# RWKV mixer: a 64x64 triangular inverse by 16x16 substitution and two joins, masks in Vector's evictions, products moved between engines

## The chip, the core and the metric

The kernel runs on one core of one Trainium2 chip. A core has five engines that run their own instruction streams and wait for each other by semaphores: TensorE (PE in the rows; its weight loads are PEld), VectorE (DVE), ScalarE (ACT), GpSimdE (POOL) and SyncE (SP), which here only issues DMA transfers. Data lie in SBUF, and matmuls write to PSUM, which has 8 banks of 128x512 fp32. The metric is the device time of one execution in microseconds; less is better.

## The reference, cut to what matters

The program is two layers of a sequence model on a 256x1024 fp32 input. Eight stages follow each other: ffn, gmlp, ffn, ple, ffn, **rwkv**, ffn, ple. Only the rwkv stage, an RWKV-7 time mixer with 16 heads of 64, is touched.

```python
dx = jnp.pad(h, ((0, 0), (1, 0), (0, 0)))[:, :-1] - h
x_rkv = h[:, :, None, :] + dx[:, :, None, :] * mu[:3]        # mixed inputs of r, k, v
r, k, v = split(einsum(x_rkv, w_in))
xw, xa, xg = h + dx * mu[3], h + dx * mu[4], h + dx * mu[5]
decay = exp(-exp(-softplus(-(w0 + tanh(xw @ w1) @ w2)) - 0.5))
a = sigmoid(a0 + (xa @ a1) @ a2)
g = sigmoid(xg @ g1) @ g2
kk = normalised per head (k * k_k);  k = k * (1 + (a - 1) * k_a)
def step(state, inp):                                         # per token
    sa = einsum('bhij,bhj->bhi', state, a_t)                  # a_t = -kk, b_t = kk * a
    state = state * w_t + sa b_t^T + v_t k_t^T
    y_t = einsum('bhij,bhj->bhi', state, r_t)
out = ((groupnorm(y) + sum(r * k * r_k) * v) * g) @ w_out
```

The kernel computes the recurrence in four chunks of 64 tokens. Inside a chunk the recurrence is a product with the inverse of a unit-triangular 64x64 matrix; there is one for each head and chunk, 64 in all.

## The kernel before

**Buffers.** SBUF holds 20 slots of 128x2048 fp32. `slot` takes one from a first-in first-out list and `drop` gives it back; `bank` and `unbank` do the same for the 8 PSUM banks. Whoever writes to a slot or bank waits until the last reader of its former content is done. The mixer's weights arrive as units of 1 MB, each a whole slot, by DMAs that SP issues in program order; `P(n, reserve)` prefetches while slots are free, `need` loads on demand. The weights of the stages around it arrive as `raw` and are split by ACT (L132) and by DVE or POOL (L134) into two parts.

**Order.** A scheduler of the framework places each instruction in its engine's stream, near the order in which the code is written. From then on each engine works strictly in that order.

**Names.** T = 256 tokens stand on the free axis of the transposed tiles (`hnT`, `kT`, `kk`, `av`, `tw`, `q2`, `bt`), the 1024 channels in 8 groups of 128 partitions. `xprod(n, ...)` (L785) makes mixed input n on DVE, in two slots that six inputs share in turn. `K` (L843) projects k, `knorm` (L864) and `kscale` (L879, POOL) make kk, `ktr` (L883) transposes k and kk, `low` (L927) makes the decay (`tw`) and the rate (`av`). `poly` (L950) turns `tw` into running decay products, two halves of 1024 columns, as a list of steps with two scans (L948) each, that the code hands out among the r projection's matmuls. POOL multiplies `bt = kk * av` (L1042) and `kT = kT * av` (L1055).

**The inverse.** `triangle(j)` (L1011, matmuls L1016) makes the off-diagonal products; their 32x32 diagonal blocks go to `md`, the blocks below to `mo`. One DVE transpose (L1061) lays them out so that each of 128 x 32 lanes has a row of its own, and `sub` (L1063) inverts the 32x32 blocks by substitution: for t = 1 to 31 a product (L1069) and a reduction (L1072), each split in up to three pieces. Two more transposes (L1229, L1232) bring the result to `wu` and `xx`. TensorE then joins the blocks to 64x64 by two sets of 64 matmuls of 32x32: q2 (L1250) and x2 (L1280).

**The v loop.** For each of 8 values of k, TensorE does four 128x512 matmuls of v (L1098) and the chunk-inner products of one channel group: 8 matmuls `sc` (L1113) and 8 `rb` (L1120). ACT copies each `sc` from its bank (L1114) and POOL multiplies it with the mask (L1115); the same for `rb` (L1122, L1124). The substitution runs beside it on DVE.

**Behind it.** `stack_v` (ACT, L1141/L1142) lays out v, `bonus` (L1149) makes r*k*v, `gate1` and `gate2` (L1190, L1208) project the gate, `tb` (L1257) transposes `bt` and `kt`. Then `chunk(c)` (L1297) runs four times: us, y, us, st, y, with gate2's eight matmuls put between.

## Time and profile before

| | us |
|---|---|
| median of 3 runs | 1233.63 (1231.42 to 1234.79) |
| the profiled execution, its own time | 1235.52 |
| its span in the trace | 1233.4 |
| TensorE busy, of the span | 1190.6 (97%) |
| VectorE busy | 805.5 (65%) |
| ScalarE busy | 610.4 (49%) |
| GpSimdE busy | 135.4 (11%) |
| mean granted TensorE clock | 0.98 |

The times in the rows count from the span's start. The mixer runs from about 750 to 980 us. TensorE is near its limit over the whole program, so the place to look at is where its busy share drops: the 40-slice line of the page shows 8, 8, 5 and 8 tenths in slices 27 to 30 (from 0), and the clock line 8, 7, 9 beside them. Every fp32 matmul leaves two records on PE, so "x64" in a row is 32 matmuls. A granted clock of 1.00 is 2.4 GHz and 0.50 is 1.2 GHz.

### The profile page before, as it was taken

The page shows a single profiled execution, that of the slowest core. Times are in us where ns is not written, and L with a number is a line of the kernel's source. Part 1 is how long each engine was busy: PE and PEld are TensorE (multiplying, and loading weights), DVE is VectorE, ACT ScalarE, POOL GpSimd, SP SyncE. Part 2 cuts the span into 40 slices and gives each one's busy share as a digit, 9 for nine tenths or more (in the row PEclk, how much of TensorE's full clock was granted, in tenths as well). Part 3 has the DMA queues.
Part 4 walks back from the last instruction along what each step waited for, and adds up shares of the span by engine and source line. Part 5 has one row for each costly group of instructions (what it writes and reads, how often), then busy time and mean ns, then how long its engine had stood idle before and what let it go on. Part 6 is the DMA issues. An engine that isn't in the chain of part 4 may idle for free.

```text
span 1233.4 us, 19738 instructions
## 1 busy us (share of the span) xinstructions
PE 1190.6 (97%) x7886; PEld 1023.4 (83%) x7886; DVE 805.5 (65%) x1214; ACT 610.4 (49%) x990; POOL 135.4 (11%) x133
## 2 busy tenths in 40 slices
PE   8999999999999999999999999988589899999997
PEld 7899998888889999987999996675357778999986
DVE  6776556696776556568656626599914988556563
ACT  7654446465574444478444412535154376444453
POOL 0000001000000000002000001343364420000011
PEclk9999999999999999999999999999879899999999
DMA  8875655565666555455656583011001358555510
GB/s 278 301 253 186 190 170 193 182 211 183 219 224 209 188 186 187 155 196 188 224 186 188 177 318 137 18 69 57 0 18 36 121 185 280 188 186 188 169 61 35
DMA packets 58780, 207.78 MB, mean 168 GB/s; under 512 B 6720, under 2 KB 7232, under 8 KB 58432
## 3 DMA queue, kind: packets, MB, share of 16 engines
q1 hardware_dynamic: 58688, 206.51, 50.4%
q8 instruction: 62, 1.02, 0.3%
q14 instruction: 30, 0.25, 0.1%
HBM read 205.44 MB, written 1.05 MB: 167 GB/s over the span
## 4 chain that ended last, share of the span: by engine, by line
PE 83%; DVE 10%; ACT 3%; issue 1%; DMA 1%; POOL 1%; SPq 0%; POOLq 0%; DVEq 0%; ACTq 0%
PE mm L157 13%; PE mm L158 13%; PE mm L156 13%; PE acc L156 8%; PE acc L157 8%; PE acc L158 8%; PE z L156 2%; PE z L157 2%; PE z L158 2%; DVE mx L1069 2%; PE k L855 2%; PE tr L253 1%; DMA raw<-in_w 1%; PE gate L156 1%; PE gate L157 1%
## 5 line engine op out<-in xcount | busy, mean ns | idle before, releaser
L134 DVE TENSOR_TENSOR w<-raw,w 128x1024 fp32r<-128x1024 f32 x335 | 408.1, 1223 | 252.6 <-ACT w L132 246.6
L132 ACT CAST w<-raw 128x1024 fp32r<-128x1024 f32 x340 | 356.6, 1052 | 319.1 <-PE mm L158 222.4
L156 PE MATMUL mm<-xT,w 128*128 128x256 f32 x1152 | 326.1, 283 | 0.0
L158 PE MATMUL mm<-xT,w 128*128 128x256 f32 x1152 | 326.0, 283 | 0.0
L157 PE MATMUL mm<-xT,w 128*128 128x256 f32 x1152 | 326.0, 283 | 0.0
L157 PEld LDWEIGHTS mm<-xT,w 128*128 128x128 f32 x1152 | 221.0, 192 | 1.3
L156 PEld LDWEIGHTS mm<-xT,w 128*128 128x128 f32 x1152 | 221.0, 192 | 1.3
L158 PEld LDWEIGHTS mm<-xT,w 128*128 128x128 f32 x1152 | 221.0, 192 | 0.0
L156 PE MATMUL acc<-w,hT 128*128 128x512 f32 x352 | 138.2, 393 | 0.0
L157 PE MATMUL acc<-w,hT 128*128 128x512 f32 x352 | 137.3, 390 | 0.0
L158 PE MATMUL acc<-w,hT 128*128 128x512 f32 x352 | 137.1, 390 | 0.0
L210 POOL TENSOR_SCALAR rpost<-ss 128x1 f32<-128x1 f32 x15 | 7.4, 494 | 790.2 <-ACT junk L217 790.2
L158 PEld LDWEIGHTS acc<-w,hT 128*128 128x128 f32 x352 | 66.1, 188 | 14.2
L156 PEld LDWEIGHTS acc<-w,hT 128*128 128x128 f32 x352 | 66.2, 188 | 12.6
L157 PEld LDWEIGHTS acc<-w,hT 128*128 128x128 f32 x352 | 66.2, 188 | 12.4
L379 DVE TENSOR_TENSOR pn<-mm,yc 128x512 f32<-128x512 f32 x72 | 47.4, 687 | 16.6 <-PE mm L158 16.6
L156 PE MATMUL mm<-w,xT 128*128 128x512 f32 x128 | 51.3, 411 | 2.3 <-ACT w L132 1.7
L157 PE MATMUL mm<-w,xT 128*128 128x512 f32 x128 | 50.9, 401 | 0.7 <-DVE xT L267 0.5
L158 PE MATMUL mm<-w,xT 128*128 128x512 f32 x128 | 50.4, 399 | 0.0
L267 DVE SCALAR_TENSOR_TENSOR xT<-tr,gT,xT 128x128 fp32r<-128x128 f32 x112 | 35.6, 345 | 22.5 <-ACT xT L266 21.8
L157 PE MATMUL z<-w,xT 128*128 128x512 f32 x128 | 49.9, 390 | 0.0
L158 PE MATMUL z<-w,xT 128*128 128x512 f32 x128 | 49.9, 390 | 0.0
(265 smaller groups left out, 1716.4 us busy)
## 6 DMA issues: line engine op xcount, KB each, us to landing
raw<-in_w SPq DMA_DIRECT2D x264, 512.0 KB, 4.2
raw<-in_win SPq DMA_DIRECT2D x32, 512.0 KB, 4.2
wf<-in_wrkv SPq DMA_DIRECT2D x12, 1024.0 KB, 5.1
raw<-in_wout SPq DMA_DIRECT2D x16, 512.0 KB, 4.3
raw<-in_wg SPq DMA_DIRECT2D x16, 512.0 KB, 3.8
gbc<-in_norm_g SPq DMA_DIRECT2D x9, 512.0 KB, 5.5
raw<-in_bwout SPq DMA_DIRECT2D x8, 512.0 KB, 3.5
bin<-in_bin SPq DMA_DIRECT2D x8, 256.0 KB, 4.4
```

The costliest lines, as they stand in the source:

```text
L132: self.high = self.nc.scalar.copy(hh, r[:p, :n])
L134: eng.tensor_tensor(ll, r[:p, :n], hh.bitcast(F32), op=ALU.subtract)
L156: mm(out, lhsT=lh, rhs=rh, start=start, stop=False)
L157: mm(out, lhsT=ll, rhs=rh, start=False, stop=False)
L158: mm(out, lhsT=lh, rhs=rl, start=False, stop=stop)
L210: nc.gpsimd.tensor_scalar(r, a, b, eps, op0=ALU.add, op1=ALU.add)
L253: nc.tensor.transpose(ps[:, k * 128:(k + 1) * 128], src[:, (k0 + k) * 128:(k0 + k + 1) * 128], self.ident)
L267: nc.vector.scalar_tensor_tensor(lo, v, gc, hi.bitcast(F32), op0=ALU.mult, op1=ALU.subtract))
L379: nc.vector.tensor_tensor(z.rearrange("p (i t) -> p i t", i=2), ps[j].rearrange("p (i t) -> p i t", i=2), rbc.unsqueeze(1).to_broadcast([1 ...
L855: mm(ps[q], lhsT=x, rhs=w[:, q * 512:(q + 1) * 512], start=k == 0, stop=k == KT - 1)
L1069: V.tensor_tensor(pr_[:, i0:i1, :t - i0], Mu[:, t, i0:t].unsqueeze(1).to_broadcast([128, i1 - i0, t - i0]), Wu[:, i0:t, i0:i1].rearrange(" ...
```

## The change

1. **Inverse.** The substitution now works on 16x16 diagonal blocks: for t = 1 to 15 one product (L1038) and one reduction (L1040) over both blocks of each 32x32 at once, through a view `diag`. The two transposes follow directly. Then TensorE joins 16 to 32: 128 matmuls q1 of 32x16, an ACT copy, 64 matmuls w1 and 128 matmuls x1 of 32x16, two kinds of additions on DVE; then 32 to 64 by q2 and x2 as before. The four parts are `join(0)` to `join(3)`, called at k = 4 to 7 of the v loop.
2. **Masks.** `inside(k)`, the chunk-inner products, runs two steps of k later than v. The mask is applied by DVE as it takes the product from PSUM (L1136, L1143); ACT and POOL have no part in it.
3. **Products.** `bt = kk * av` (L1017, two of 1024 columns) and `kT = kT * av` (L1107) run on DVE. r is copied out of PSUM by ACT into a slot `rT` (L1101), and its four banks are renamed for v (`rebank`).
4. **Mixed inputs.** Each has its own slot and is made whole: 1 in `start`, 3 in K(0), 4 after K(1), 0 after knorm(0), 2 and 5 in the code after the r loop (the scheduler places 2 within the second half of the decay chain). Prefetches in K, low and the r loop are gone: r's last unit and v's four are loaded on demand, into slots that fall free then.
5. **Order.** ktr takes kk first, all copies on ACT; `squares` and `decay` replace `poly`, the triangles stand directly behind; both `tb` groups and `bonus` come after the v loop, all four `stack_v` after the copies of v, and gate1's eight steps are filled in from there on.

On DVE, from the transpose at the substitution's start, there stood before (mx and wu are the blocks and the result, kT the bonus' product):

```order
L1061 STREAM_TRANSPOSE wu_7330<-mx_7456 128x1024
L1084 TENSOR_TENSOR kT_7328<-kT_7328,r_7460 128x512
L1069 TENSOR_TENSOR mx_7456<-wu_7330 128x1 x3
L1072 TENSOR_REDUCE wu_7330<-mx_7456 128x1 x3
L1069 TENSOR_TENSOR mx_7456<-wu_7330 128x2x2 x3
L1072 TENSOR_REDUCE wu_7330<-mx_7456 128x2 x3
```

And at the end of the substitution there now stand, also on DVE (pn is the product, sk the operand of the chunks, mk the mask):

```order
L1038 TENSOR_TENSOR pn<-wu_7333 128x450
L1136 TENSOR_TENSOR sk_7743<-sc_7786,mk 64x512
L1040 TENSOR_REDUCE wu_7333<-pn 128x2x15
L1136 TENSOR_TENSOR sk_7743<-sc_7792,mk 64x512
L1041 STREAM_TRANSPOSE wu_7333<-wu_7333 128x32x32
L1042 STREAM_TRANSPOSE mx_7469<-wu_7333 128x32x32
L1136 TENSOR_TENSOR sk_7743<-sc_7812,mk 64x512
L1136 TENSOR_TENSOR sk_7743<-sc_7818,mk 64x512
L1143 TENSOR_TENSOR rb_7764<-rb_7785,mk 128x512
```

One product and one reduction per t take the place of up to three each, they end at t = 15, and mask evictions stand among and behind them.

On PE, in the v loop before, a step of k was:

```order
L1098 MATMUL v_7711<-wf_7630,xr_7533 128x512
L1098 MATMUL v_7712<-wf_7630,xr_7533 128x512
L1098 MATMUL v_7713<-wf_7630,xr_7533 128x512
L1098 MATMUL v_7714<-wf_7630,xr_7533 128x512
L1113 MATMUL sc_7980<-sk_7690,q_481_7355 64x128 x4
L1113 MATMUL sc_7987<-sk_7690,q_481_7355 64x128 x4
L1120 MATMUL rb_7979<-sk_7690,bt_7455 64x64 x8
```

Now, on PE in steps 4 and 5 of the v loop (q_534 is q1, w_538 and x_537 are w1 and x1):

```order
L1135 MATMUL sc_7844<-sk_7744,q_480_7360 64x128 x4
L1141 MATMUL rb_7837<-sk_7744,bt_7468 64x64 x8
L1050 MATMUL q_534_7858<-wu_7333,nq_7591 32x16 x128
L1153 MATMUL v_7765<-wf_7810,xr_7715 128x512
L1153 MATMUL v_7766<-wf_7810,xr_7715 128x512
L1153 MATMUL v_7767<-wf_7810,xr_7715 128x512
L1153 MATMUL v_7768<-wf_7810,xr_7715 128x512
L1135 MATMUL sc_7992<-sk_7744,q_480_7360 64x128 x4
L1135 MATMUL sc_7998<-sk_7744,q_480_7360 64x128 x4
L1141 MATMUL rb_7837<-sk_7744,bt_7468 64x64 x8
L1057 MATMUL w_538_8014<-nq_7591,mx_7469 32x16 x64
L1060 MATMUL x_537_8013<-mx_7469,nq_7591 32x16 x128
```

The 320 small matmuls of the new join stand between the steps of v. On PE in chunk 0 there stood before, from its second us on:

```order
L1333 MATMUL us_8385<-k_8395,xx_8100 64x64 x8
L1345 MATMUL st_8397<-sv_8091,bn_8218 64x64 x8
L1345 MATMUL st_8409<-sv_8091,bn_8218 64x64 x8
L1357 MATMUL y_8374<-sv_8091,rb_7715 64x64 x8
L1208 MATMUL g_579_8472<-wf_7852,gl_8132 128x512
```

and now:

```order
L1339 MATMUL us_8601<-k_8611,xx_8332 64x64 x8
L1351 MATMUL st_8613<-sv_8456,bn_8468 64x64 x8
L1351 MATMUL st_8627<-sv_8456,bn_8468 64x64 x2
L1231 MATMUL g_571_8565<-xr_7724,wf_8566 128x256
L1231 MATMUL g_571_8565<-xr_7724,wf_8566 32x256 x2
```

gate1's sixteen matmuls (g_571) moved from before the chunks into chunk 0, behind most of its st. The diff, cut to this:

```diff
+            if n not in X["x"]:
+                X["x"][n] = self.slot("xr")
             hv, dv = g8(X["hnT"]), g8(X["dxT"])
...
+            for k in ks:
+                V.scalar_tensor_tensor(xent(n, k)[:, lo:hi], dv[:, k, lo:hi], mu(n, k), hv[:, k, lo:hi], op0=ALU.mult, op1=ALU.add)
...
                     start(1)
-                    for pr in range(4):
-                        xprod(1, pr, 128, 256)
+                    xprod(3)
...
-                    xprod(4, k // 2)
-                    P(1, 8)
-            if b:
-                knorm(0, p0)
...
+        squares(0)
+        knorm(1, p1)
         ktr(0)
-        step(1)
+        low(0, 2)
+        low(0, 3)
...
         self.release(at["l"])
+        ktr(1)
...
+        for i in range(2):
+            if i:
+                squares(i)
+            decay(i)
+            V.tensor_tensor(bt[:, hs(i)], kk[:, hs(i)], av[:, hs(i)], op=ALU.mult)
+            ab(i)
+            triangle(i)
+        self.drop(eo)
+        nq = self.slot("nq")
+        nx, qn = blk(nq[:, :1024]), blk(nq[:, 1024:])
+        G.memset(nq, 0.0)
+        S.copy(nx[:, :, 16:32], blk(md)[:, :, 16:32])
...
+            return bass.AP(t.tensor, t.offset, [list(t.ap[0]), [528, 2], [32, 16], [1, 16]])
+        Wd, Md = diag(zt), diag(wu_[:, 1024:])
+        for t in range(1, 16):
+            pr_ = self.small(512, "pn", 3)[:, :2 * t * t].rearrange("p (a i s) -> p a i s", a=2, i=t)
+            V.tensor_tensor(pr_, Md[:, :, t, 0:t].unsqueeze(2).to_broadcast([128, 2, t, t]),
+                            Wd[:, :, 0:t, 0:t].rearrange("p a s i -> p a i s"), op=ALU.mult)
+            V.tensor_reduce(Wd[:, :, t, 0:t], pr_, axis=AX.X, op=ALU.add)
+        V.transpose(wv.rearrange("p n s -> p s n"), Wu.rearrange("p t s -> p s t"))
+        V.transpose(xt.rearrange("p n t -> p t n"), Wu)
+        def join(i):
+            if i == 0:
+                ps = self.bank("q1")
+                for n in range(32):
+                    for o in range(0, 128, 32):
+                        mm(ps[o:o + 32, n * 16:(n + 1) * 16], lhsT=nx[o:o + 16, n, :], rhs=wv[o:o + 16, n, 0:16], start=True, stop=True)
+                S.copy(qn[:, :, 0:16], ps.rearrange("p (n t) -> p n t", t=16))
+                self.unbank(ps)
+            elif i == 1:
+                ps, pw = self.bank("x1"), self.bank("w1")
+                for n in range(32):
+                    for o in (0, 64):
+                        mm(pw[o:o + 32, n * 16:(n + 1) * 16], lhsT=xt[o:o + 32, n, :], rhs=qn[o:o + 32, n, 0:16], start=True, stop=True)
+                for n in range(32):
+                    for o in range(0, 128, 32):
+                        mm(ps[o:o + 32, n * 16:(n + 1) * 16], lhsT=qn[o:o + 32, n, :], rhs=xt[o:o + 32, n, 16:32], start=True, stop=True)
+                for o in (0, 64):
+                    V.tensor_tensor(wv[o:o + 32, :, 0:16], pw[o:o + 32].rearrange("p (n t) -> p n t", t=16), wv[o:o + 32, :, 0:16], op=ALU.add)
+                V.tensor_tensor(xt[:, :, 16:32], ps.rearrange("p (n t) -> p n t", t=16), xt[:, :, 16:32], op=ALU.add)
+                self.unbank(pw, ps)
...
+            elif i == 2:
+                for hh in range(2):
+                    ps = self.bank("q2")
+                    for i in range(16):
+                        n = hh * 16 + i
+                        for o in (0, 64):
+                            mm(ps[o + 32:o + 64, i * 32:(i + 1) * 32], lhsT=mo[o:o + 32, n * 32:(n + 1) * 32],
+                               rhs=wv[o:o + 32, n, :], start=True, stop=True)
+                    for o in (0, 64):
+                        (S.copy if o else V.tensor_copy)(qv[o + 32:o + 64, hh * 16:hh * 16 + 16, :], ps[o + 32:o + 64].rearrange("p (n t) -> p n t", t=32))
+                    self.unbank(ps)
+            else:
+                for o in range(0, 128, 32):
+                    c0 = o // 32 % 2 * 32
+                    (V.tensor_copy if c0 else S.copy)(xv[o:o + 32, :, c0:c0 + 32], xt[o:o + 32])
+                for hh in range(2):
+                    ps = self.bank("x2")
+                    for i in range(16):
+                        n = hh * 16 + i
+                        for o in (0, 64):
+                            mm(ps[o:o + 32, i * 32:(i + 1) * 32], lhsT=qv[o + 32:o + 64, n, :], rhs=xt[o + 32:o + 64, n, :], start=True, stop=True)
+                    for o in (0, 64):
+                        (S.copy if o else V.tensor_copy)(xv[o:o + 32, hh * 16:hh * 16 + 16, 32:64], ps[o:o + 32].rearrange("p (n t) -> p n t", t=32))
+                    self.unbank(ps)
...
-            if k == 0:
-                ktr(1)
-                for i in range(4):
-                    sl = slice(i * 512, (i + 1) * 512)
-                    G.tensor_tensor(bt[:, sl], kk[:, sl], av[:, sl], op=ALU.mult)
-            if k:
-                step(2)
-            if k == 6:
-                triangle(0)
-            if k > 3:
-                xprod(2, k - 4)
-            P(1, 2)
-        step(99)
-        self.drop(eo)
-        triangle(1)
+        self.drop(X["x"][0])
+        rT = self.slot("rT")
+        for g in range(4):
+            S.copy(rT[:, g * 512:(g + 1) * 512], psr[g])
+        for n in (2, 5):
+            xprod(n)
+        self.drop(hnT, dxT)
...
-        G.tensor_tensor(kT, kT, av, op=ALU.mult)
+        V.tensor_tensor(kT, kT, av, op=ALU.mult)
...
-        def sub(t0, t1):
-            for t in range(t0, t1):
-                cut = [0] + [c for c in (8, 16) if c < t] + [t]
-                part = list(zip(cut, cut[1:]))
-                for i0, i1 in part:
-                    V.tensor_tensor(pr_[:, i0:i1, :t - i0], Mu[:, t, i0:t].unsqueeze(1).to_broadcast([128, i1 - i0, t - i0]),
-                                    Wu[:, i0:t, i0:i1].rearrange("p s i -> p i s"), op=ALU.mult)
-                for i0, i1 in part:
-                    L["sub"] = V.tensor_reduce(Wu[:, t, i0:i1], pr_[:, i0:i1, :t - i0], axis=AX.X, op=ALU.add)
...
-        psv = [[self.bank("v") for _ in range(2)] for _ in range(NB)]
+                V.tensor_tensor(skv[g][half[h], :, h, :, 64:128], gs(rT, g)[half[h]], gs(gam, g)[half[h]], op=ALU.mult)
+        V.tensor_tensor(kT, kT, rT, op=ALU.mult)
+        self.drop(gam, ta, rT)
...
+        def inside(k):
+            g, m = k // 2, k % 2
+            if m == 0:
+                X["rb"] = self.bank("rb")
+            psb = X["rb"].rearrange("p (m c t) -> p m c t", m=2, c=4)
+            for h in range(2):
+                hh, ho = half[h], half[1 - h]
+                ps = self.bank("sc")
+                pv = ps.rearrange("p (c t) -> p c t", c=4)
+                for c in range(NCH):
+                    mm(pv[ho, c], lhsT=c4(kt)[hh, k, c], rhs=skv[g][hh, m, h, c, :], start=True, stop=True)
+                V.tensor_tensor(skv[g][ho, m, h], pv[ho], mk[ho].unsqueeze(1).to_broadcast([64, 4, 128]), op=ALU.mult)
+                self.unbank(ps)
+            for c in range(NCH):
+                for h in range(2):
+                    hh = half[h]
+                    mm(psb[hh, m, c], lhsT=c4(bt)[hh, k, c], rhs=skv[g][hh, m, h, c, 64:128], start=True, stop=True)
+            if m:
+                V.tensor_tensor(c3(rb_[:, g * 512:(g + 1) * 512]), c3(X["rb"]), mk[:, 64:128].unsqueeze(1).to_broadcast([128, 8, 64]), op=ALU.mult)
+                self.unbank(X["rb"])
...
+        psv = [[self.rebank(psr[2 * b + q], "v") for q in range(2)] for b in range(NB)]
...
-            sub(*((1, 9), (9, 12), (12, 15), (15, 17), (17, 19), (19, 21), (21, 23), (23, 24))[k])
             if k in (1, 3):
                 P(1, 0)
+            if k > 1:
+                inside(k - 2)
             if k > 3:
-                xprod(5, k - 4)
-            g, m = k // 2, k % 2
...
-                S.copy(skv[g][ho, m, h], pv[ho])
-                G.tensor_tensor(skv[g][ho, m, h], skv[g][ho, m, h], mk[ho].unsqueeze(1).to_broadcast([64, 4, 128]), op=ALU.mult)
...
-            if m:
-                S.copy(rb_[:, g * 512:(g + 1) * 512], psb)
-                a = c3(rb_[:, g * 512:(g + 1) * 512])
-                G.tensor_tensor(a, a, mk[:, 64:128].unsqueeze(1).to_broadcast([128, 8, 64]), op=ALU.mult)
-                self.unbank(psb)
-        sub(24, 32)
-        self.drop(hnT, dxT)
-        self.drop(xr[0])
+                if k == 7:
+                    self.drop(X["x"][2])
+                    xx = self.slot("xx")
+                    xv = xx.rearrange("p (n t) -> p n t", t=64)
+                    for o in (32, 96):
+                        G.memset(xv[o:o + 32, :, 0:32], 0.0)
+                join(k - 4)
+        inside(6)
+        inside(7)
...
-        stack_v(0)
-        stack_v(1)
+        for c in range(NCH):
+            stack_v(c)
...
-        wv, qv = blk(wu_[:, 1024:]), blk(md)
-        V.transpose(wv.rearrange("p n s -> p s n"), Wu.rearrange("p t s -> p s t"))
-        xx = self.slot("xx")
-        xv = xx.rearrange("p (n t) -> p n t", t=64)
-        V.transpose(xv[:, :, 0:32].rearrange("p n t -> p t n"), Wu)
-        for o in (32, 96):
-            L["xc"] = S.copy(xv[o:o + 32, :, 32:64], xv[o:o + 32, :, 0:32])
-            G.memset(xv[o:o + 32, :, 0:32], 0.0)
-        with behind("xc"):
-            stack_v(2)
-            stack_v(3)
         fill.extend(lambda k=k: gate1(k) for k in range(KT))
-        bonus()
...
-        for hh in range(2):
-            filler(3)
-            for h in range(2):
-                o = h * 64
...
-        for i in range(2):
-            filler(1)
-            for g in range(2):
-                tb(0, i, g)
-        for hh in range(2):
-            for h in range(2):
-                filler(1)
-                tb(1, hh, h)
...
-                    mm(ps[o:o + 32, i * 32:(i + 1) * 32], lhsT=qv[o + 32:o + 64, n, :], rhs=xv[o + 32:o + 64, n, 32:64], start=True, stop=True)
-                (S.copy if h else V.tensor_copy)(xv[o:o + 32, hh * 16:hh * 16 + 16, 32:64], ps[o:o + 32].rearrange("p (n t) -> p n t", t=32))
-                self.unbank(ps)
-        self.drop(bt, kt)
+        for b in range(NB):
+            for i in range(2):
+                for g in range(2):
+                    tb(b, i, g)
+        bonus()
         filler(8)
+        self.drop(bt, kt, nq)
         fill.extend(lambda b=b, q=q, i=i: gate2(b, q, i) for b in range(NB) for q in range(2) for i in range(2))
```

## Rows read from the trace of the kernel before

**Rows 1.** Windows: length, PE, PEld, DVE, ACT, POOL busy (count), granted clock, DMA share, GB/s.

```profile
880.00:900.00 20.00, 5.46 (x39) 3.34 (x38) 13.45 (x31) 6.34 (x10) 4.41 (x4) 0.66 0.00 1
796.00:944.00 148.00, 124.38 (x1104) 85.55 (x1102) 109.30 (x234) 61.64 (x115) 59.08 (x38) 0.88 0.11 38
```

**Rows 2.** Timeline of PE around the v loop: start, us, line, operation, count, idle before.

```profile
834.30 3.68 PE L1016 MATMUL m<-kk,bt 64*64 64x64 f32 x64 [5.71 <-DVE wu L1059]
845.65 3.70 PE L1098 MATMUL v<-wf,xr 128*128 128x512 f32 x8
850.88 3.70 PE L1098 MATMUL v<-wf,xr 128*128 128x512 f32 x8
896.28 1.32 PE L1113 MATMUL sc<-sk,q 64*64 64x128 f32 x5 [14.54 <-ACT sk L1114]
```

**Rows 3.** Windows of line L1069 alone, then of L1072 alone, on DVE.

```profile
848.00:894.00 46.00, 30.66 (x69) 0.92 0.07 24
848.00:894.00 46.00, 14.34 (x69) 0.92 0.07 24
```

**Rows 4.** Timeline of DVE, 799 to 848.

```profile
799.74 1.22 DVE L959 SCALAR_TENSOR_TENSOR q<-eo 128x1024 f32<-128x1024 f32 x1
812.89 6.61 DVE L948 TENSOR_TENSOR_SCAN q<-eo,wu 128x1024 f32<-128x1024 f32 x1
826.01 2.28 DVE L948 TENSOR_TENSOR_SCAN tw<-q,wu 128x1024 f32<-128x1024 f32 x1
838.28 1.38 DVE L1083 TENSOR_TENSOR sk<-r,tw 64x512 f32<-64x512 f32 x2
845.70 2.00 DVE L1061 STREAM_TRANSPOSE wu<-mx 128x1024 f32<-128x1024 f32 x1
```

**Rows 5.** Timeline of POOL beside the slow scan.

```profile
812.53 4.81 POOL L1055 TENSOR_TENSOR kT<-kT,a 128x2048 f32<-128x2048 f32 x1 [1.20 <-ACT a L1054]
```

**Rows 6.** Windows of the three stretches of low clock, columns as in Rows 1.

```profile
834.00:840.00 6.00, 5.70 (x68) 4.40 (x68) 5.97 (x12) 5.83 (x12) 0.00 (x0) 0.62 0.00 1
896.00:918.00 22.00, 20.05 (x130) 10.51 (x130) 0.68 (x1) 11.15 (x20) 15.25 (x10) 0.68 0.07 21
930.00:936.00 6.00, 6.00 (x96) 5.06 (x93) 0.83 (x2) 3.62 (x8) 1.64 (x1) 0.72 0.25 90
```

**Rows 7.** Groups by form on DVE, 845 to 895: count, busy us, mean ns.

```profile
L1069 DVE TENSOR_TENSOR mx<-wu 128x248 f32<-128x248 f32 x1 | 0.6, 569 | 0.0
L1069 DVE TENSOR_TENSOR mx<-wu 128x1 f32<-128x1 f32 x3 | 0.3, 155 | 0.0
L1072 DVE TENSOR_REDUCE wu<-mx 128x8 f32<-128x248 f32 x1 | 0.4, 406 | 0.0
L1072 DVE TENSOR_REDUCE wu<-mx 128x2 f32<-128x4 f32 x3 | 0.3, 148 | 0.0
```

**Rows 8.** Timeline of PE, the r projection and what stands in it.

```profile
796.74 3.72 PE L1034 MATMUL r<-xr,wf 128*128 128x256 f32 x16
800.29 1.91 PE L889 MATMUL tr<-ident,kn 128*128 128x128 f32 x16
802.04 20.89 PE L1034 MATMUL r<-xr,wf 128*128 128x256 f32 x96
822.86 2.08 PE L1016 MATMUL m<-kk,bt 64*64 64x64 f32 x64
```

**Rows 9.** Timeline of PE, small matmuls of the joins.

```profile
909.01 3.43 PE L1250 MATMUL q<-wu,mx 32*32 32x32 f32 x64
918.04 2.11 PE L1250 MATMUL q<-wu,mx 32*32 32x32 f32 x64
```

**Rows 10.** Timeline of ACT behind the v loop.

```profile
896.74 1.06 ACT L1132 COPY vn<-v 128x512 f32<-128x512 f32 x2
902.69 0.72 ACT L1142 ACTIVATE sv<-vn,ck 64x512 f32<-64x512 f32 x1
```

**Rows 11.** DMA issues: count, KB each, median us from issue to landing.

```profile
wf<-in_g SPq DMA_DIRECT2D x1, 1024.0 KB, 5.4
```

149 lines of the change are left out of this document (51 added, 98 removed).

## The prediction

> **What bounds the kernel now.** I read the windows first, then the timelines of PE and DVE in the mixer. Over the program TensorE is busy 97% of the span, so only stretches where it is not can pay. In the 20 us from 880 PE is busy 5.46 us [rows 1]: it waits 14.54 us before the last `sc` of the v loop, for a bank that ACT's copy holds [rows 2]. ACT is named, but it waits itself for the substitution on DVE, whose products and reductions take 30.66 + 14.34 = 45.0 us between 848 and 894 [rows 3]. A second wait, 5.71 us, stands before the second triangle [rows 2]: there DVE's decay chain is late. Part of that lateness is POOL's: the scan beside POOL's 4.81 us product takes 6.61 us, the one without it 2.28 [rows 4, 5].
>
> I make the sum on PE, from 796 to 944: before the first, r starts; at 944, chunk 1 starts. Of these 148 us PE is busy 124.4 [rows 1], so 23.6 are idle: 5.7 and 14.5 as above, and 3.4 in short waits. The three stretches at a low granted clock cost, busy time by the share of the clock that is missing [rows 6], 5.70 x 0.38 + 20.05 x 0.32 + 6.00 x 0.28 = 10.3 us. What is left, 148 - 23.6 - 10.3 = 114.1 us, is the work itself at 2.4 GHz, and the change removes none of it; it adds to it.
>
> **DVE after the change.** One product cost 155 ns at 1 element and 569 at 248 [rows 7], so 1.67 ns an element; a reduction 148 ns at 4 and 406 at 248, so 1.06 ns. Over t = 1 to 15 there are 2 x t x t elements, 2480 in all: products 15 x 0.155 + 4.1 = 6.5 us, reductions 15 x 0.145 + 2.6 = 4.8. So 11.3 us stand for 45.0. Against that DVE takes over POOL's products (two of 1024 columns at about the 1.14 us from start to start that its 1.22 us operation of that width shows, and one of 2048, 2.2 us [rows 4]) and the masks: 16 of 64x512 and 4 of 128x512, about 0.65 us each by the 0.69 of such a product [rows 4].
>
> In time: the decay chain starts near 793.4, and each half takes some 15 us (four operations and three products at 1.14, two scans at 2.28, mixed inputs between), so its halves end near 808.3 and 823.5. Then eight mixed inputs 3.2, kT 2.2, transpose 2.0, kt x kT 2.2: the substitution starts near 833.1. With it in the stream stand eight `sk` products (5.2), the bonus' product (2.2) and two masks (1.3), and behind it two transposes (3.8): 833.1 + 11.3 + 8.7 + 3.8 = 856.9, where before the transposes began at about 890. Three more mask evictions, 2.0 us, free the bank that q1 needs: 858.9.
>
> **PE after the change.** Sixteen transposes, 1.91, now stand ahead of r, which starts near 798.6. A step of r costs 16 x 20.89 / 96 = 3.5 us [rows 8]. Two steps bring PE to 805.6; the first triangle waits until 808.3, 2.7 us. A triangle is 2.08 us [rows 8], three steps 10.5, so PE is at 820.9 and waits 2.6 us until 823.5 for the second. r ends near 836.1. A step of v with its inside products is 5.23 us from start to start, 3.63 without them [rows 2]; five steps and three groups of inside products end at 859.1. So PE and DVE come to the join together: the 14.5 us wait goes, **and PE bounds the rest**.
>
> The new join issues 128 + 64 + 128 matmuls, 640 records. No row has a 32x16 matmul. The nearest, q2's 32x32, took 2.11 / 64 = 33 ns a record at full clock and 3.43 / 64 = 54 at half [rows 9]; a 64x64 triangle, with four times the area, took 2.08 / 64 = 33 too [rows 8]. If columns decide, 16 of them cost half, 16.5 ns; if issue decides, 33, and in a stretch of low clock at most 54. I take 33, since 32 and 64 columns cost the same: 640 x 0.033 = 21.1 us. At 16.5 it is 10.6.
>
> Waits that come in: the two triangles, 5.3 us. After v, ACT has four copies at 0.53 and eight stack copies at 0.73 in its stream, 8.0 us [rows 10], ahead of its evictions of x2, whose banks the last `sc` need; PE has 6.7 us of work meanwhile, so it waits about 2.5 us with the second bank. Bounds: nothing, if those evictions are taken earlier, and 8.0. g1's weights can be requested only when the bonus' matmul has read its slot, and 1 MB took 5.4 us to land [rows 11]; PE has about 5 us of chunk 0 first: 1.0 us, between 0 and 7.5 if g1 queues behind another transfer. Bank before q1: 0.3. Together 9.1 us. v's first units are requested near 826.7 and wanted at 836.1 and 843.4, so they are covered; if that cover failed, a load would cost up to 5.4.
>
> **The clock.** It fell while PE was idle for 5.71 us; what came after ran at a mean 0.62 [rows 2, 6], 2.2 us lost. It also fell to a mean of 0.72 in 930 to 936 with PE busy 6.00 of 6.00 [rows 6], behind a stretch of 32x32 matmuls. q1 is 8.4 us of still smaller matmuls, w1 and x1 12.6. I count one such loss behind each: 2 x 2.2 = 4.4 us. Bounds: none, and the clock of 1.2 GHz kept through all of it (rival C).
>
> The Trainium skill ("TensorE: Matmul & The Clock Gate", HAM oscillation) asks for matmul bursts without idle gaps to keep the fast clock; the row of 930 to 936 speaks against taking that as enough for tiny tiles. By the rule the 4.4 us would not be lost, and the time would be 1230.
>
> **The sum.** 114.1 + 21.1 + 9.1 + 4.4 = 148.7 us for what took 148.0: +0.7. What follows, chunks 1 to 3 and the output, keeps its instructions and the weight stream. The profiled execution, 1235.5 us, becomes 1236.2; it lay 1.9 over the median of 1233.63, so I forecast a median of **1234**. In short: DVE's 37 us are gained, but what PE gains by it, 23.6 of idle time and 10.3 of low clock, is spent on the new matmuls (21.1) and on new waits.
>
> **The rivals.**
>
> A, the forecast: 1231 to 1238, chance 0.40.
>
> B, the join is cheaper, in one of two ways. Matmuls of 16 columns cost half as much as those of 32: 10.5 us less, 1223.7. For it: the cost at half clock, 54 against 33, shows that part of it is in cycles; against it: 64 columns cost no more than 32. Or the clock holds: 1230. For it: q2's second group ran at 33 ns, thus at full clock, inside the join of before. Both: 1219. Chance 0.32. The Trainium skill (same page, "Wait — 56ns, not 53.3ns?") puts the least distance from start to start at about 25 ns; an estimate by that is 640 x 25 = 16.0 us, 5.1 less than mine, 1229. No row here shows 25.
>
> C, slower: the tiny matmuls hold the clock at 1.2 GHz from q1 to the end of v. The place is steps 5 to 7 of the v loop: three v groups cost 3.63 us more each and their inside products about 1.3 more, 14.8 in all, of which 4.4 are counted: +10.4, **1245**. If the 640 records also go at 54 ns it is 13.4 more. It decides as soon as two more dense pieces start at half clock. For it: 896 to 918 ran at 0.68 although PE was busy 20.05 of 22 us. Against it: there PE had just been idle. Chance 0.20.
>
> D, what is loaded on demand comes late: r's last unit, v's or g1, each up to 5.4 us and a clock loss of 2.2 behind it: 1240 to 1242. For it: the prefetches are gone. Against it: the slots are free some 5 us before the data are wanted, and more for v's later units. Chance 0.08.
>
> **How the numbers follow.** A measurement of this kernel tells about 0.3% from no change: below 1229.9 is faster, above 1237.3 slower. Faster: 0.28 of B and 0.04 of A, 0.32. Slower: C, most of D and 0.03 of A, 0.30. Same: 0.38. The range leaves out the cheapest ends of B and the dearer half of C: 1219 to 1247.
>
> **What would show it.** In the profile of the changed kernel: DVE's two transposes end near 857; PE waits two to three microseconds at each triangle; q1's 256 records take 8.4 us (4.2 by B); the granted clock falls to 0.50 in v's steps 5 and 6 and comes back (stays, by C); the ACT queue stands before the last `sc`; g1 starts within chunk 0 behind a DMA; chunk 1 starts near 945, by B at 930 to 940, by C at 955. It is wrong if chunk 1 comes at its time but the end does not, since then the tail has changed, which I cost at nothing because its instructions are the same.

## The result, and the profile after

The changed kernel takes 1224.30 us (median of 4 runs, 1223.71 to 1225.68) where the kernel before takes 1233.82 (1231.42 to 1234.79): a ratio of 0.9927 with a 95% interval of 0.991 to 0.9945. It is faster by 9.5 us. The forecast of no change was wrong; the time lies in rival B's region, inside the range. The profiled execution took 1224.77 us with a span of 1223.0.

The windows of the changed kernel, all engines (columns as in [rows 1]). The first is the stretch on which the sum was made; it now ends at 932, since chunk 1 starts at 932.25 instead of 943.96.

```profile
796.00:932.00 136.00, 124.68 (x1740) 88.14 (x1739) 89.33 (x147) 53.37 (x103) 18.46 (x12) 0.91 0.16 57
874.00:886.00 12.00, 8.99 (x255) 5.57 (x254) 2.96 (x5) 3.03 (x3) 0.00 (x0) 0.58 0.02 4
```

TensorE is busy as long as before (124.7 us against 124.4 of [rows 1]) with 636 more records in it, and idle for 11.3 us instead of 23.6. The second window shows that the clock did fall in the new join.

Timeline of PE in the changed kernel, what answers to [rows 2, 8, 9] (start, us, line, count, and in brackets the idle time ahead with its releaser; "issue" means that the profile shows nothing that PE waited for):

```profile
798.16 7.07 PE L1094 MATMUL r<-xr,wf 128*128 128x256 f32 x32
...
807.99 2.84 PE L1002 MATMUL m<-kk,bt 64*64 64x64 f32 x64 [2.75 <-DVE kk L976]
...
823.00 2.08 PE L1002 MATMUL m<-kk,bt 64*64 64x64 f32 x64 [0.80 <-DVE wu L1028]
...
835.48 10.46 PE L1153 MATMUL v<-wf,xr 128*128 128x512 f32 x24
...
859.43 2.13 PE L1050 MATMUL q<-wu,nq 16*32 16x16 f32 x179
...
863.19 1.25 PE L1050 MATMUL q<-wu,nq 16*32 16x16 f32 x77 [1.64 <-issue]
...
864.37 5.02 PE L1153 MATMUL v<-wf,xr 128*128 128x512 f32 x8
...
871.28 2.14 PE L1057 MATMUL w<-nq,mx 32*32 32x16 f32 x125 [0.29 <-DVE sk L1136]
...
874.91 1.91 PE L1060 MATMUL x<-mx,nq 32*32 32x16 f32 x128 [1.33 <-issue]
...
878.91 1.79 PE L1060 MATMUL x<-mx,nq 32*32 32x16 f32 x118 [2.10 <-issue]
...
880.63 5.42 PE L1153 MATMUL v<-wf,xr 128*128 128x512 f32 x8
...
887.58 2.21 PE L1071 MATMUL q<-wu,mx 32*32 32x32 f32 x128
...
894.96 2.21 PE L1085 MATMUL x<-mx,wu 32*32 32x32 f32 x128
...
899.09 0.76 PE L1135 MATMUL sc<-sk,q 64*64 64x128 f32 x5 [0.82 <-ACT xx L1087]
...
916.22 9.38 PE L1231 MATMUL g<-xr,wf 128*128 128x256 f32 x32
...
932.25 1.15 PE L1312 MATMUL us<-sv,sk 128*64 128x64 f32 x32
```

The 14.54 us wait of [rows 2] is gone. q1 runs from 859.43 to 864.37, w1 and x1 from 871.28 to 880.63: 4.94 + 9.35 = 14.3 us for 640 records, of which 1.64 + 1.33 + 2.10 = 5.1 are gaps inside the groups. Without the gaps a record takes 9.2 / 640 = 14 ns, and most of these records ran at the low clock. q2's 128 records take 2.15 us to the next v, 17 ns each, where [rows 9] has 33 for the same tile.

On DVE, groups of the changed kernel from 832 to 857, what answers to [rows 3] (count, busy us, mean ns):

```profile
L1038 DVE TENSOR_TENSOR pn<-wu 128x2 f32<-128x2 f32 (+14 forms) x15 | 6.7, 445 | 0.5
...
L1040 DVE TENSOR_REDUCE wu<-pn 128x2 f32<-128x2 f32 (+14 forms) x15 | 4.8, 321 | 0.3
```

And its timeline, what answers to [rows 4]:

```profile
803.23 2.28 DVE L950 TENSOR_TENSOR_SCAN q<-eo,wu 128x1024 f32<-128x1024 f32 x1
...
852.96 2.10 DVE L1041 STREAM_TRANSPOSE wu<-wu 128x1024 f32<-128x1024 f32 x1
854.96 1.87 DVE L1042 STREAM_TRANSPOSE mx<-wu 128x1024 f32<-128x1024 f32 x1
```

The substitution takes 11.5 us where it took 45.0, all scans take 2.28, and the transposes end at 856.83. That is the predicted time of Vector to the tenth; what was wrong lies on TensorE.

### The profile page after: what moved, and what is told of

Same layout as the page of the kernel before. It is cut to its first block, busy times and chain, and to the rows that moved or that the text cites. A ratio compares the mean times of both kernels' runs of the same rounds, so it can differ in the third digit from the quotient of the medians.

```text
span 1223.0 us, 20881 instructions
## 1 busy us (share of the span) xinstructions
PE 1191.8 (97%) x8526; PEld 1027.2 (84%) x8526; DVE 786.3 (64%) x1129; ACT 603.6 (49%) x978; POOL 97.1 (8%) x109
## 5 line engine op out<-in xcount | busy, mean ns | idle before, releaser
L165 PEld LDWEIGHTS acc<-w,hT 128*128 128x128 f32 x352 | 66.3, 188 | 12.4
L165 PE MATMUL z<-w,xT 128*128 128x512 f32 x128 | 49.9, 390 | 0.0
L166 PE MATMUL z<-w,xT 128*128 128x512 f32 x128 | 49.9, 390 | 0.0
L164 PE MATMUL z<-w,xT 128*128 128x512 f32 x128 | 49.7, 393 | 0.0
```

The costliest lines, as they stand in the source:

```text
L164: mm(out, lhsT=lh, rhs=rh, start=start, stop=False)
L165: mm(out, lhsT=ll, rhs=rh, start=False, stop=False)
L166: mm(out, lhsT=lh, rhs=rl, start=False, stop=stop)
```

## The experiments

Times are medians, with the ratio to the kernel before and its 95% interval; the kernel before ran beside each group at 1233.3 to 1234.3 us. "Later" and "earlier" without a word are against the changed kernel's 1224.3.

### What the order of the tiles' rows is worth

**e1** puts the row half outermost again in q2 and x2:

```diff
-                    for i in range(16):
-                        n = hh * 16 + i
-                        for o in (0, 64):
+                    for o in (0, 64):
+                        for i in range(16):
+                            n = hh * 16 + i
```

> The changed kernel, but q2 and x2 take all 16 matmuls of one row half before those of the other, as the kernel before did; nothing else. Theory (neighbours in different row groups of the array overlap): a record goes back from 17 ns to 32 to 35 ns, the two times 128 records from 2.15 us each to 4.2 to 4.5, and the end comes 3 to 5 us later. Rival (small matmuls were cheap for another reason, such as a clock that had risen): records stay at 17 ns and the end within 1 us.

1230.61 us, ratio 0.9973 (0.9961 to 0.9985): 6.3 later, more than the theory's 3 to 5. PE in e1:

```profile
886.72 3.93 PE L1071 MATMUL q<-wu,mx 32*32 32x32 f32 x128
...
897.51 4.15 PE L1085 MATMUL x<-mx,wu 32*32 32x32 f32 x128
```

31 and 32 ns a record instead of 17. The two joins themselves take 3.6 us longer; besides, the clock loses more: busy time by the missing share of clock, up to chunk 1, is 12.7 us in e1 and 9.6 in the changed kernel. It falls to 0.50 as q2 ends (890.8) and in x2 (901.0), with TensorE busy all the time since each of them began.

**e2** puts the row group outermost in q1, w1 and x1, where the change alternates four groups (two in w1):

```diff
-                for n in range(32):
-                    for o in range(0, 128, 32):
+                for o in range(0, 128, 32):
+                    for n in range(32):
```

> The changed kernel, but q1, w1 and x1 take all matmuls of one row group before those of the next. Theory (overlap of different row groups): a record costs 25 to 33 ns instead of 11 to 16, and since TensorE then asks for instructions more slowly the three waits of 1.3 to 2.1 us with no named cause inside q1, w1 and x1 go; the 640 records take 16 to 21 us with no such gap instead of 14.3 with gaps, the end comes 2 to 7 us later. Rival 1 (16 columns cost half of 32): records stay at 11 to 17 ns and the end within 1 us. Rival 2 (the gaps have another cause than the rate of instructions): records dearer and the gaps stay, the end 7 to 12 us later.

1240.03 us, ratio 1.0053 (1.0033 to 1.0074): 15.7 later, and slower than before. PE in e2:

```profile
859.61 12.16 PE L1050 MATMUL q<-wu,nq 16*32 16x16 f32 x256
...
883.53 13.09 PE L1060 MATMUL x<-mx,nq 32*32 32x16 f32 x253
```

That is 47 and 52 ns a record, x1 wholly and q1 mostly at the low clock; the first 1.6 us of q1 ran at full clock, at about 32 ns a record. In [rows 9] a tile twice as wide took 54 and 33. So the number of columns does not decide, nor does a count of instructions: the same instructions in the same number cost 14 or 50 ns by the order of their rows.

The gaps marked "issue" are gone, as the theory said, but the end comes later than even the second rival's 7 to 12, because of the clock. It falls within q1 and again within w1, with TensorE busy without a gap, and loses 18.7 us by the same count. Windows of PE in e2, before and after the fall in q1 (length, busy, clock, DMA share, GB/s):

```profile
859.60:861.20 1.60, 1.60 (x54) 1.00 0.00 0
861.30:874.90 13.60, 13.60 (x212) 0.50 0.01 2
```

**e11** makes the same edit as the change, alternation in q2 and x2, in the kernel before, and nothing else:

```diff
-            for h in range(2):
-                o = h * 64
-                ps = self.bank("q2")
-                for i in range(16):
-                    n = hh * 16 + i
+            ps = self.bank("q2")
+            for i in range(16):
+                n = hh * 16 + i
+                for o in (0, 64):
```

> The kernel before with one edit: in the two joins with q2 and x2 the two row halves alternate from one matmul to the next, in one bank for both halves, as in the changed kernel; nothing else. Theory (tiles in different rows overlap, and these joins are on the path): both joins together take 4.3 us instead of 8 to 9, and the time falls by 3 to 6.3 us: 1227.5 to 1231. Rival (in the kernel before filler matmuls stand between the joins, and what waits for the copies behind them is no earlier): under 1.5 us, 1232 to 1234.5.

1226.67 us, ratio 0.9928 (0.99 to 0.9956): 7.6 under the kernel before, more than the top of the theory (6.3). The first group of each join in e11 (there are two of each), on PE:

```profile
909.63 1.20 PE L1249 MATMUL q<-wu,mx 32*32 32x32 f32 x64
...
920.41 1.20 PE L1280 MATMUL x<-xx,mx 32*32 32x32 f32 x64
```

In the traces both joins together take 4.5 us from start to start, in the kernel before 9.9. Besides, the clock stays at 1.00 from 905 on in e11, where the kernel before has it low up to 918 and again in 930 to 936 [rows 6]; the loss up to chunk 1 is 4.9 us by the count above instead of 10.7. So the gain is the cheaper records and the clock that does not fall again. This one edit is nearly as fast as the whole change; the two intervals overlap.

### The gaps and the clock

**e3** spreads q1 over v's step 5 in four parts, and w1 and x1 over step 6; **e4** lets `sc`, `st` and `y` alternate their halves too:

```diff
+                    if n % 8 == 7 and n < 31:
+                        yield
...
+                    next(part, None)
```

> The changed kernel, but q1 is given out in four parts behind the four matmuls of v's step 5, and w1 and x1 likewise in step 6, instead of standing in one block ahead of the step. Theory (the gaps of 5.1 us in all come from a stream of instructions that runs dry, and the loss of 3.2 us in v's steps 5 and 6 from the clock that falls in these gaps): with a 0.9 us matmul between the parts both go, the end comes 5 to 9 us earlier. Rival 1 (changing between small and full tiles costs as much): the end within 2 us. Rival 2 (the clock falls because of small tiles, gaps or no gaps): gaps go, the clock falls all the same, the end 2 to 5 us earlier.

> The changed kernel, but sc in the inside products, and y and st in the chunks, alternate between the two halves from matmul to matmul as us and rb do already. Theory (neighbours on different row or column groups overlap): the 16 sc records of a step go from about 83 to 45 ns, 0.6 us a step and 4 to 5 us in eight steps, y and st from 56 to 34 ns a record, 2 to 3 us in each of the first chunks; the end comes 5 to 12 us earlier, less where the chunks wait for evictions and not for TensorE. Rival (the order is of no account for tiles of 64): no difference above 1 us.

e3: 1222.09 us (ratio 0.9906, 0.989 to 0.9922), 2.2 earlier, under the theory's gain and, as the intervals overlap, not clear of zero. Two of three gaps are closed and behind q1 the clock no longer falls. One gap remains, though v's matmuls stand between the parts there too; 2.0 us after it the clock falls, so that q2 runs slower:

```profile
862.60 0.73 PE L1050 MATMUL q<-wu,nq 16*32 16x16 f32 x64
...
877.70 0.55 PE L1063 MATMUL x<-mx,nq 32*32 32x16 f32 x44 [0.99 <-issue]
...
883.50 3.62 PE L1076 MATMUL q<-wu,mx 32*32 32x32 f32 x128
```

e4: 1224.1 us (ratio 0.992, 0.9905 to 0.9936), no difference. A step's `sc` takes 0.76 us instead of 1.25, but PE then waits for DVE's masks (1.34, 0.60 and 0.29 us in its trace, 1.08 in the changed kernel) and longer for ACT ahead of the last `sc` and in the bonus; it is idle for 13.4 us up to chunk 1 instead of 11.3. In the chunks the same happens: chunk 1 takes 11.55 us instead of 13.45, and chunk 2 takes 13.9 instead of 11.0, with a wait during which the clock falls. PE in e4:

```profile
952.77 0.47 PE L1352 MATMUL st<-sv,bn 128*64 128x64 f32 x2 [3.84 <-ACT sv L1342]
```

What TensorE saved beside busy evictions was waited away.

### Whether the new inverse pays

**e5** keeps all else of the change, but runs the old 32x32 substitution on DVE in the v loop, and no q1, w1, x1:

```diff
-                join(k - 4)
+            sub(*((1, 9), (9, 12), (12, 15), (15, 17), (17, 19), (19, 21), (21, 23), (23, 24))[k])
...
+        sub(24, 32)
...
+        join(2)
+        join(3)
```

> The changed kernel, but the inverse as before: substitution of the 32x32 blocks on DVE (products and reductions for t = 1 to 31, given out along the v loop), then q2 and x2 in the changed kernel's alternating order behind the v loop; no q1, w1, x1. Masks, products and mixed inputs stay as changed. Theory (the join takes 34 us off DVE, and TensorE pays 14.3 us of small matmuls and about 3 us of low clock for it): DVE's stream of substitution and mask evictions ends near 900 instead of 857, TensorE waits for it some 10 to 20 us and then runs at 1.2 GHz for a while; the end comes 5 to 10 us later than the changed kernel. Rival (with POOL's products gone the old substitution would have been quick enough, and what pays is the order of q2 and x2 and the gate in chunk 0): between 3 us earlier and 2 us later.

1215.84 us (1215.22 to 1221.37), ratio 0.9864 (0.9829 to 0.9898): 8.5 us **earlier** than with the new inverse. My theory fell. The end of the v loop in e5, on DVE and on PE:

```profile
877.99 2.06 DVE L1162 STREAM_TRANSPOSE wu<-wu 128x1024 f32<-128x1024 f32 x1
879.93 1.90 DVE L1163 STREAM_TRANSPOSE mx<-wu 128x1024 f32<-128x1024 f32 x1
...
882.70 1.30 PE L1134 MATMUL sc<-sk,q 64*64 64x128 f32 x5 [4.54 <-DVE sk L1135]
```

The old substitution now ends at 881.8, 11.7 us earlier than in the kernel before, whose transposes ended at 893.5. It starts at 832.0 instead of 848, and its 69 products take 20.0 us instead of the 30.66 of [rows 3], since POOL no longer multiplies masks beside them (e14 below tests this). PE waits 4.54 us for it, not 14.54. To save that wait the new inverse gives TensorE 14.3 us of join, and the clock loses 9.6 us with it and 5.6 without. It relieved an engine which the rest of the change had already made nearly early enough.

### Products and masks: on Vector or on Pool

**e7** puts `bt` and `kT` back on Pool in the changed kernel, **e10** moves them to Vector in the kernel before, **e13** is e5 with them on Pool:

```diff
-        V.tensor_tensor(kT, kT, av, op=ALU.mult)
+        G.tensor_tensor(kT, kT, av, op=ALU.mult)
```

> The changed kernel, but bt = kk x av (four pieces of 512 columns) and kT = kT x av are POOL's again. Theory (they stand on DVE's chain to the substitution, and POOL needs about 2.0 us where DVE needs 0.6, and slows DVE beside it): both triangles and the substitution start later, TensorE waits more, 2 to 6 us later. Rival (POOL works beside the scans and DVE's stream gets 4.5 us shorter): 0 to 3 us earlier.

> The kernel before with one edit: the products kk*av (in two halves) and kT*av on Vector instead of Pool. Theory (Pool's products hold Vector, and Vector holds the second triangle): beside Pool's 8.0 us of kk*av and 4.8 us of kT*av Vector lost about 0.8 + 1.1 + 1.1 + 4.3 = 7.3 us (the scans of 3.04 and 6.61 for 2.28, a wait of 1.09, a 16-wide scaling of 1.24 for 0.17); it pays 2.4 us for kk*av ahead of the triangles, so the second triangle's wait of 5.71 us shrinks to about 1 and the time falls by 4 to 7 us: 1227 to 1230. Rival (what the undoing of this edit in the changed kernel cost, 11.6 us, comes from that kernel's order, not from the products): within 2 us of before, 1232 to 1236.

> The changed kernel with the 32x32 substitution on Vector again (1215.8 us so far) and, besides, the products kk*av and kT*av back on Pool. Theory (what pays in the changed kernel is the earlier start of the substitution, and the products on Vector are what makes it early in this order of the work): 8 to 12 us later, 1224 to 1228, about the kernel before with alternating halves in the joins. Rival (as in the kernel before, where moving the products alone changed nothing, Vector pays as much as it wins): 1214 to 1218.

e7: 1235.93 us, ratio 1.0013 (1.0001 to 1.0026), 11.6 later, about twice what I expected; the whole gain is gone. e10: 1234.09, ratio 1.0002 (0.9984 to 1.002), nothing, as its rival said. e13: 1222.84 (1218.85 to 1224.94), ratio 0.9909 (0.9878 to 0.9941), 7.0 later than e5, by the two intervals just not clear of zero; the theory's 8 to 12 is just missed, and all five runs lie above the rival's 1214 to 1218. The timeline of e7, of POOL, DVE and PE:

```profile
820.12 4.59 POOL L1109 TENSOR_TENSOR kT<-kT,a 128x2048 f32<-128x2048 f32 x1 [13.47 <-ACT a L1108]
...
820.25 4.49 DVE L967 TENSOR_SCALAR gC<-tw 128x16 f32<-128x16 f32 x1
...
811.60 3.68 PE L1002 MATMUL m<-kk,bt 64*64 64x64 f32 x64 [6.95 <-DVE kk L976]
...
829.71 3.20 PE L1002 MATMUL m<-kk,bt 64*64 64x64 f32 x64 [4.46 <-DVE wu L1030]
```

A 16-wide scaling that takes 0.17 us alone takes 4.49 and ends with Pool's product. Both triangles wait for Vector, 11.4 us instead of 3.6, and run at the low clock behind it. In e10 the mechanism is there as well: scans back at 2.28, the second triangle's wait down from 5.71 to 1.39 us. But the last wait stays, as the timeline of PE and ACT shows:

```profile
832.89 2.08 PE L1016 MATMUL m<-kk,bt 64*64 64x64 f32 x64 [1.39 <-DVE wu L1059]
...
896.93 5.68 PE L1154 MATMUL bo<-kT,hsel 128*16 128x256 f32 x16 [14.88 <-ACT sk L1114]
...
895.23 1.04 ACT L1234 COPY xx<-xx 32x1024 f32<-32x1024 f32 x1 [18.38 <-DVE xx L1232]
```

There Vector is busy from the decay chain to the end of the substitution (80 of 84 us from 796 to 880), so 4.6 us of products taken over cost it nearly what the contention gave back. With its r loop 2.9 us later in this execution (799.65 against 796.74), its transposes end 1.2 us earlier than before, and chunk 1 no earlier. What moves with the products depends on what stands beside them: in the changed order the first triangle comes early and TensorE waits directly for the products; in the old one it did not.

**e6** and **e14** give the masks back to an ACT copy and a Pool product, in the changed kernel and in e5:

```diff
-                V.tensor_tensor(skv[g][ho, m, h], pv[ho], mk[ho].unsqueeze(1).to_broadcast([64, 4, 128]), op=ALU.mult)
+                S.copy(skv[g][ho, m, h], pv[ho])
+                G.tensor_tensor(skv[g][ho, m, h], skv[g][ho, m, h], mk[ho].unsqueeze(1).to_broadcast([64, 4, 128]), op=ALU.mult)
```

> The changed kernel, but the inside products leave PSUM by ACT copies and POOL multiplies them by the mask, as before. Theory (with the substitution ended near 857 the masks are hidden on either engine): DVE loses about 13 us of work, ACT's copies of the last two steps stand behind the copies of v, the end is 0 to 3 us later. Rival 1 (POOL beside DVE slows both, and the banks are held by ACT): 4 us or more later. Rival 2 (DVE's mask evictions hold up q1): 1 to 3 us earlier.

> The same kernel with the 32x32 substitution on Vector, products on Vector, but the masks as in the kernel before: a copy on ScalarE and a product on Pool. Theory (Vector ends the stretch of v, where TensorE waits 4.5 us for it at the end, and the masks are 16 x 0.69 + 4 x 0.67 = 13.7 us of its work there): 3 to 6 us earlier, 1209 to 1213. Rival (Pool's products hold Vector for as long as Vector would have worked on the masks): 1214 to 1218.

e6: 1226.32 us (ratio 0.9935, 0.9913 to 0.9958), 2.0 later, within the theory, but by the intervals not clear of zero. e14: 1224.65 (0.9928, 0.9903 to 0.9953), 8.8 *later* than e5 where my theory wanted 3 to 6 earlier, worse than the rival too. The substitution's products and reductions in e5 (groups on DVE, 832 to 895):

```profile
L1038 DVE TENSOR_TENSOR mx<-wu 128x144 f32<-128x144 f32 (+28 forms) x69 | 20.0, 335 | 0.1
L1041 DVE TENSOR_REDUCE wu<-mx 128x1 f32<-128x1 f32 (+29 forms) x69 | 14.5, 255 | 0.0
```

The same of e14:

```profile
L1038 DVE TENSOR_TENSOR mx<-wu 128x1 f32<-128x1 f32 (+29 forms) x69 | 28.7, 462 | 0.0
L1041 DVE TENSOR_REDUCE wu<-mx 128x1 f32<-128x1 f32 (+31 forms) x69 | 14.4, 257 | 0.0
```

And the timeline of ACT and PE in e14:

```profile
883.92 2.10 ACT L1078 COPY xx<-mx 32x1024 f32<-32x1024 f32 x2 [16.51 <-DVE mx L1166]
...
886.68 1.32 PE L1134 MATMUL sc<-sk,q 64*64 64x128 f32 x5 [10.51 <-ACT sk L1135]
```

Two things undo the saving. Of the 13.7 us of masks, 8.2 stood ahead of the transposes in e5; beside Pool the same 69 products take 28.7 us instead of 20.0, 8.7 more, while the reductions, with one operand, stay. So the transposes end 84.1 us after r's start, in e5 84.5. And the `sc` copies now stand behind ACT's copies of the inverse, which wait for the transposes: PE waits 10.51 us, in the same form as the 14.54 in [rows 2].

### Versions that beat both

**e9b** is the changed kernel with q1, w1, x1 and q2 spread over v's steps 5 to 7, `sc`, `st` and `y` alternating, x2's copies on DVE, gate1's widths changing every other step, the triangles one r step later and the bonus' product behind the substitution. **e12** takes the same with the old substitution (no joins to spread); **e12b** is e12 with triangles and bonus product where the change has them; **e15** is e12b with the masks of `sc` on ACT and Pool; those of `rb` stay on Vector.

> The changed kernel with what the first runs point to: q1, w1, x1 and q2 given out among the matmuls of v's steps 5 to 7 in parts of 32, sc, y and st alternating between halves, x2 copied by DVE alone and so not behind ACT's copies of v, the triangles one step of r later, the gate's two widths in an order with half the changes of width. Theory: 2 to 4 us from the spreading, 2 from sc where TensorE sets the pace, 1 from x2, 2 to 4 from the triangles (no wait and no low clock behind it), 1 from the gate: 6 to 11 us earlier than the changed kernel, 1213 to 1218. Rival (DVE's chain sets the start of the join and the chunks wait for evictions, so that what TensorE saves before and behind it turns into waiting): 2 to 4 us, 1220 to 1222.

> The 32x32 substitution on Vector again (no q1, w1, x1), with all else of the changed kernel, plus what the tuned version with the new inverse had: sc, y and st alternate their row halves, x2's copies on Vector, the gate's widths change every other step, the triangles one r step later, kT*rT off the front of the substitution. Theory (the new inverse costs more on TensorE than it frees on Vector, and the rest adds up): 1207 to 1212, below the 1214.2 of the tuned version with the new inverse and 1215.8 of the old substitution alone. Rival (with the old substitution Vector ends the v stretch, so what TensorE saves there is waited away): 1213 to 1217.

> As the kernel just ahead, but the triangles and kT*rT stand where the changed kernel has them. Theory (Vector ends the v stretch, so the 2.3 us of kT*rT ahead of the substitution's longer steps count): 1 to 3 us later than the kernel ahead. Rival (the later second triangle delays the substitution's start by as much as the product gave back): within 1 us of it or earlier.

> As the kernel just ahead, with alternating row halves in sc, x2's copies on Vector and the gate's widths changing every other step (the 1214.3 us version with its masks on ScalarE and Pool). Theory: 3 to 6 us earlier than with masks on Vector, 1208 to 1211. Rival: 1213 to 1217.

e9b: 1214.18 us, ratio 0.9835 (0.9811 to 0.9859), as its theory said. e12: 1220.79 (0.9878, 0.9848 to 0.9908), later than its theory and its rival. e12b: 1214.31 (0.9833, 0.9807 to 0.9859), earlier than e12, as its rival said. e15: 1219.55 (0.9887, 0.9847 to 0.9926), later than its theory and its rival. Windows of PE in e9b (length, busy, clock, DMA share, GB/s):

```profile
796.00:924.00 128.00, 120.39 (x1750) 0.97 0.17 60
860.00:890.00 30.00, 30.00 (x950) 1.00 0.02 4
```

And one part of q1 in its timeline:

```profile
863.68 0.73 PE L1029 MATMUL q<-wu,nq 16*32 16x16 f32 x64
```

Between v's matmuls the small ones go without gaps, at 10 ns each from one group's start to the next (0.65 us for 64), and the clock stays at 1.00 from 860 to 890. In e12 the theory failed: the later triangles let the old substitution start 2.5 us later than in e12b (834.65 against 832.16), PE waits 3.70 us for a mask, and the clock loss of the stretch is 14.6 us by the same count against 9.6 in e12b. e15 repeats e14: the masks of `sc` on Pool cost 5.2 us. The two inverses end level, 1214.2 and 1214.3, each after its own tuning. For the old one the tuning is worth 1.5 us over e5, not clear of zero; for the new one it is worth 10.1, and the runs do not show which of its edits gives it.

## Why the prediction was wrong

**What bounds the kernel before** held: the wait of 14.54 us stands behind the old substitution. e10 and e11 moved other things and kept it (14.88, 14.59). But I set 11.3 us against 45.0 as if the 45.0 were the substitution's own. In e5 it takes 34.5 with the masks off POOL and starts 16 us earlier, and 10 of the 14.5 us of wait go without any new inverse.

**Vector after the change** held to the tenth: transposes end at 856.83 (856.9 predicted), the substitution takes 11.5 us (11.3), q1 starts at 859.43 (859.1), r at 798.16 (798.6). The first triangle waits 2.75 us (2.7); the second 0.80 (2.6), since the first ran at the low clock, 2.84 us, and PE came later.

**The sum** failed, in two terms of the work. From 796 to chunk 1 it forecast 148.7 us; it took 136.25. By the same count (busy less busy time at the missing share of clock, which also books the records at low clock at half), the work is 125.0 - 9.6 = 115.3 us against 114.1 + 21.1 = 135.2. Of these 115.3 us, the new join's records are 6.2 and the rest 109.1.

- *The join, 21.1 us.* It took 14.3 on the clock of the trace, 5.1 of it gaps, which stand below among the waits. The price of 33 ns came from q2's row in the kernel before [rows 9]; there one row half follows itself. The change's loops run over the row groups innermost, which stood in the diff, and I did not ask what that does. e2 shows that it is worth 15.7 us, clock included. Without the gaps a record took 14 ns, under the lower bound of 16.5, and I chose between columns and issue when it was neither.
- *"The change removes none" of the 114.1 us.* It does: q2 and x2 now alternate their halves, 2.15 us each, where at full clock the old order takes 4.2 for q2 (2 x 2.11) and 4.7 for x2 (four groups of 1.2). I called these joins as before and read only the new ones. That is 4.6 us of the 5.0 by which the rest of the work came out under 114.1. e11 shows that this edit alone is worth 7.6 us, e1 that its undoing costs 6.3, both with what the clock adds.

**The clock** was counted at 4.4 us and lost 9.6: 1.7 at the first triangle, 2.6 from q1 on, 3.6 from the end of w1 on, 1.7 behind the wait before the last `sc`. It fell to 0.50 in steps 5 and 6 and came back, as said. The idle gaps in the join are not the cause by themselves: q1's fall comes 0.8 us into q1, before its gap, as windows of PE in the changed kernel show, and e2 has two falls and no gap in its joins.

```profile
859.40:860.20 0.80, 0.80 (x97) 1.00 0.00 0
860.30:861.50 1.20, 1.20 (x97) 0.50 0.05 14
```

**The waits** were 9.1 us, measured 11.3, in other places: triangles 3.6 (5.3), bank 1.1 (0.3), ACT's queue 0.8 (2.5), others 0.7, and 5.1 of gaps inside the new joins, which I had not foreseen. No load was late: g1 began at once in chunk 0, and D did not happen. Together: -19.8 of work, +5.2 of clock, +2.2 of waits make the 12.4 us by which chunk 1 came before its forecast. Behind it the tail was 1.3 us longer (1223.0 - 932.25 against 1233.4 - 943.96).

**Rival B** had the right side and place (chunk 1 at 930 to 940, q1 4.94 us where B said 4.2), but not by its reasons: 16 columns are no cheaper than 32 in the same order (e2), and the clock did not hold. The Trainium skill ("TensorE: Matmul & The Clock Gate", Wait — 56ns, not 53.3ns?) puts the least distance from start to start at about 25 ns. The prediction took a record for a matmul, though a matmul leaves two. Here 179 records of q1 took 2.13 us, 12 ns each, and e9b's 10, so 20 to 24 ns a matmul, less than that floor in either count; the measurement decides. The same page's Part 3, Packing small matmuls, says that small tiles overlap when their row groups differ, and that was the section to read: 31 against 17 ns (e1 and the changed kernel, q2) and 47 against 12 (e2 and the changed kernel, q1) agree with it.

**Rival C** was right that the clock falls in the joins, wrong that it stays; in e2, where the records are dearer, it stays at 0.50 for 13.6 us and for 20.4.

**What the gain is made of.** "DVE's 37 us are gained" was true and beside the point. From the kernel before: alternating joins alone, -7.6 us (e11); with the new order and masks on Vector, -3.8 more (e13); products on Vector, -7.0 more (e5, 1215.8); the new inverse, +8.5 (1224.3). Each of these times has an interval of some 2 to 4 us to either side, so that the step of -3.8 is not shown, that of -7.0 is at the edge, and the first and the last are clear. The steps also depend on their order: products are worth 0 (e10), 7.0 (e13) or 11.6 (e7), masks 2.0 (e6, not clear of zero) or 8.8 (e14). I did not ask what the change gives *without* its largest edit.

## What to carry to other kernels

Before small matmuls are priced, look at which rows of the array follow each other: the price from a row of a like tile in another order was wrong by a factor of two to four. Ask of a change with several edits what each gives if the largest is left out; an edit that relieves the named bottleneck can cost more than the wait that the others leave. Pool's two-operand products beside a busy Vector are paid by Vector, and a copy on ACT behind one that waits stops TensorE in another engine's name.
